# Four loads for six at the end of a row-sum kernel

## The chip, the cores and the metric

The kernel runs on one core of one Trainium2 chip. The metric is the device time of one execution in microseconds (us), taken over several executions.

## The reference

```python
x = randn(32, 512, 1024), float32
out = sum(maximum(x, 0), axis=-1)      # shape (32, 512), float32
```

There are 16,384 rows of 1024 columns, 67.1 MB to read and 0.07 MB to write. Each row is clamped at zero and summed.

## The kernel before

Each of the 128 partitions has 128 rows of its own. Seven loads of 16 rows a partition (8.4 MB each) fill three buffers in turn. The scalar engine (ACT) clamps and the vector engine (DVE) sums. The last 16 rows come in smaller loads, so that little work is left after the last byte. All loads go out on one queue, that of SyncE (SP). Each load has a semaphore, a counter that reaches 16 when all 16 DMA engines have finished their part of the load; an instruction that uses the data waits for 16. That moment is called the landing here.

The parts that the change and the argument touch, with cuts marked:

```python
TAIL = [8, 4, 2, 1]                  # rows of the tail loads, then the last row in pieces:
PIECES = [244, 252, 260, 268]        # columns
# ... cut ...
    extra = len(PIECES) - 1
    parts = [                        # the last piece has room for the sums of the others
        nc.alloc_sbuf_tensor(f"piece{i}", [P, w + extra * (i == extra)], F32)
        for i, w in enumerate(PIECES)
    ]
# ... cut: load() issues on SP and counts up a semaphore of its own by 16; act_row() and
#     dve_row() clamp and sum one row with accum_out, waiting for `loaded` where given ...
    for n in TAIL:
        loaded = load(
            buf[:, c : c + n, :], rows(m, n), None if c else freed[NB - NBUF]
        )
        for i in range(n):           # rows alternate between ACT and DVE
            if i % 2 == 0 or (n == 8 and i == 7):
                act_row(buf[:, c, :], m, loaded if i == 0 else None)
            else:
                dve_row(buf[:, c, :], res[:, m : m + 1], loaded if i == 1 else None)
            c += 1
            m += 1
    col = 0
    arrived = []
    for part, w in zip(parts, PIECES):
        arrived.append(load(part[:, :w], rows(m, 1)[:, 0, col : col + w]))
        col += w

    store(0, ROWS, *freed[0])
    store(ROWS, NT - ROWS - 2, n_act - 1, n_dve)

    last, w = parts[-1], PIECES[-1]
    for i in range(extra):           # the sum of piece i goes into column w + i of the last piece
        dve_row(parts[i][:, :], last[:, w + i : w + i + 1], arrived[i])
    nc.vector.wait_ge(arrived[-1], 16)          # L203: a separate wait instruction
    before_last = n_dve
    nc.vector.tensor_scalar(                    # L205: the last piece and the three sums
        out=last[:, :], in0=last[:, :], scalar1=0.0, scalar2=None,
        op0=MAX, op1=ADD, accum_out=res[:, NT - 1 : NT],
    ).wait_op(sems.dve, before_last, "sem-ge").then_inc(sems.dve, 1)
    n_dve += 1
    store(NT - 2, 2, n_act, n_dve)
```

The last DVE instruction has two things to wait for: the last load and DVE's own earlier sums. The kernel puts the first into an instruction of its own and the second on the instruction itself.

Of the kernel before, what the change touches and what calls it, by code (L numbers as in the profile page):

```python
# [4 lines left out]
F32 = mybir.dt.float32  # L5
RELU = mybir.ActivationFunctionType.Relu
MAX, ADD = mybir.AluOpType.max, mybir.AluOpType.add
P = 128

ROWS = 16  # L10
# [3 lines left out]
TWO = [[16], [16], [16], [8, 8], [8, 8], [7, 7], []]  # L14
ACT = [0, 0, 0, 0, 0, 2, 9]
DVE = [0, 0, 0, 0, 0, 0, 7]

TAIL = [8, 4, 2, 1]
PIECES = [244, 252, 260, 268]

EARLY = 1

# [1 line left out]
def kernel(tc: tile.TileContext, x: bass.AP, out: bass.AP):  # L24
    nc = tc.nc
    sems = Semaphores(tc)

    tc.close()
    tc.compile()
    nc.cur_bb = nc.bb_map[tc.start_bb_name]  # L30
    body = nc.cur_bb.bb.instructions
    ends = list(body)
    body.clear()
    n_stores = relu_sum(nc, sems, x, out)
    body.extend(ends)


    nc.cur_bb = nc.bb_map[tc.start_bb_name + "_end"]
    body = nc.cur_bb.bb.instructions
    clear = semaphore_clear(body)  # L40
    body.clear()
    nc.gpsimd.wait_ge(sems.stored, 16 * n_stores)
    body.extend(clear)
    issue_ahead_of_the_barrier(tc, EARLY)


class Semaphores:
    def __init__(self, tc: tile.TileContext):
        n = len(TWO) + len(TAIL) + len(PIECES)
        self.loads = [tc.alloc_semaphore(f"load{i}") for i in range(n)]  # L50
        self.act = tc.alloc_semaphore("act")
        self.dve = tc.alloc_semaphore("dve")
        self.stored = tc.alloc_semaphore("stored")


def relu_sum(nc, sems: Semaphores, x: bass.AP, out: bass.AP):
    x_flat = x.flatten_outer_dims()
    N, D = x_flat.shape
    NT = N // P
    NB = len(TWO)  # L60
    assert N == P * NT == P * ROWS * (NB + 1)
    assert sum(TAIL) == ROWS - 1 and sum(PIECES) == D

    bufs = [nc.alloc_sbuf_tensor(f"io{i}", [P, ROWS, D], F32) for i in range(NBUF)]
    res = nc.alloc_sbuf_tensor("res", [P, NT], F32)
    extra = len(PIECES) - 1
    parts = [
        nc.alloc_sbuf_tensor(f"piece{i}", [P, w + extra * (i == extra)], F32)
        for i, w in enumerate(PIECES)
    ]  # L70


# [7 lines left out]
    def rows(m, n):  # L80
        if m < ROWS:
            return xf[:, m : m + n, :]
        return xv[:, m - ROWS : m - ROWS + n, :]

    def sums(m, n):
        if m < ROWS:
            return of[:, m : m + n], res[:, m : m + n]
        return ov[:, m - ROWS : m - ROWS + n], res[:, m : m + n]
# [3 lines left out]
    def load(dst, src, after=None):  # L92
        nonlocal n_load
        dma = nc.sync.dma_start(out=dst, in_=src)  # L94
        if after:
            dma.wait_op(sems.dve, after[1], "sem-ge")
        dma.then_inc(sems.loads[n_load], 16)
        n_load += 1
        return sems.loads[n_load - 1]

    def store(m, n, act, dve):
        nonlocal n_store
        dst, src = sums(m, n)
        nc.sync.wait_ge(sems.act, act)
        nc.sync.dma_start(out=dst, in_=src).wait_op(sems.dve, dve, "sem-ge").then_inc(
            sems.stored, 16
        )
        n_store += 1
# [16 lines left out]
    def act_row(ap, m, loaded):  # L125
        nonlocal n_act
        i = nc.scalar.activation(  # L127
            out=ap, in_=ap, func=RELU, accum_out=res[:, m : m + 1]
        )
        if loaded is not None:  # L130
            i.wait_op(loaded, 16, "sem-ge")
        i.then_inc(sems.act, 1)
        n_act += 1

    def dve_row(ap, accum_out, loaded):
        nonlocal n_dve
        i = nc.vector.tensor_scalar(  # L137
            out=ap,
            in0=ap,
            scalar1=0.0,  # L140
            scalar2=None,
            op0=MAX,
            op1=ADD,
            accum_out=accum_out,
        )
        if loaded is not None:
            i.wait_op(loaded, 16, "sem-ge")
        i.then_inc(sems.dve, 1)
        n_dve += 1

    freed = []
    m = 0
    for j in range(NB):
        buf = bufs[j % NBUF]
        loaded = load(buf[:, :, :], rows(m, ROWS), j >= NBUF and freed[j - NBUF])
        c = 0
# [19 lines left out]
    buf = bufs[NB % NBUF]  # L176
    c = 0
# [4 lines that stand above are left out]
        for i in range(n):  # L182
# [3 lines left out]
                dve_row(buf[:, c, :], res[:, m : m + 1], loaded if i == 1 else None)  # L186
            c += 1
            m += 1
    col = 0
    arrived = []  # L190
    for part, w in zip(parts, PIECES):
        arrived.append(load(part[:, :w], rows(m, 1)[:, 0, col : col + w]))
        col += w



    store(0, ROWS, *freed[0])
    store(ROWS, NT - ROWS - 2, n_act - 1, n_dve)

    last, w = parts[-1], PIECES[-1]  # L200
    for i in range(extra):
        dve_row(parts[i][:, :], last[:, w + i : w + i + 1], arrived[i])
    nc.vector.wait_ge(arrived[-1], 16)  # L203
    before_last = n_dve
    nc.vector.tensor_scalar(  # L205
# [3 lines left out]
        scalar2=None,  # L209
        op0=MAX,  # L210
        op1=ADD,
        accum_out=res[:, NT - 1 : NT],
    ).wait_op(sems.dve, before_last, "sem-ge").then_inc(sems.dve, 1)
    n_dve += 1
    store(NT - 2, 2, n_act, n_dve)
# [59 lines left out]
```

## Time and profile before

| | before |
|---|---|
| time, median of 3 runs | 162.18 us (162.17 to 162.97) |
| span in the profile | 160.06 us |
| DVE busy / ACT busy | 74% / 65% |
| DMA packets | 2592, 67.18 MB |

The table of stretches gives, for each stretch, its length, the busy time of DVE, ACT and POOL, then the clock, the busy share of the 16 DMA engines (which can read slightly above 1 in this view) and GB/s. Near the end of before:

```profile
151.00:152.00 1.00, 1.00 (x3) 1.00 (x3) 0.00 (x0) 1.00 0.97 410
153.00:154.00 1.00, 1.00 (x3) 1.00 (x3) 0.00 (x0) 1.00 0.97 410
155.00:156.00 1.00, 0.96 (x1) 0.99 (x2) 0.00 (x0) 1.00 1.02 372
```

In these stretches the DMA engines are busy all the time; DVE and ACT nearly are too, but with work that the loads have just brought.

The timeline of DVE at the end (start, duration, line, instruction, and in brackets idle time before it with what ended it; the long instructions clamp and sum, the short ones that follow read out the sum):

```profile
156.72 0.41 DVE L137 TENSOR_SCALAR_CACHE_REDUCE piece<-piece 128x244 f32<-128x244 f32 x1 [0.44 <-DMA piece<-in_x_dram]
157.05 0.08 DVE L137 DVE_READ_ACCUMULATOR piece<-piece 128x1 f32 x1
157.08 0.42 DVE L137 TENSOR_SCALAR_CACHE_REDUCE piece<-piece 128x252 f32<-128x252 f32 x1
157.42 0.08 DVE L137 DVE_READ_ACCUMULATOR piece<-piece 128x1 f32 x1
157.45 0.43 DVE L137 TENSOR_SCALAR_CACHE_REDUCE piece<-piece 128x260 f32<-128x260 f32 x1
157.80 0.09 DVE L137 DVE_READ_ACCUMULATOR piece<-piece 128x1 f32 x1
157.92 0.43 DVE L205 TENSOR_SCALAR_CACHE_REDUCE piece<-piece 128x271 f32<-128x271 f32 x1
158.28 0.08 DVE L205 DVE_READ_ACCUMULATOR piece<-piece 128x1 f32 x1
```

And the end of the chain of waits (start, duration, what), followed back from the last instruction ("issue" is time in which the engine waited for nothing that the profile shows):

```profile
127.86 28.83 DMA piece<-in_x_dram
156.69 0.02 issue
156.72 1.18 DVE piece L137 x6
157.90 0.03 issue
157.92 0.44 DVE piece L205 x2
```

The chain runs through the first piece's landing and then through DVE alone. The semaphore records of the trace tell when each load has landed on all 16 DMA engines: the four pieces at 156.69, 157.06, 157.43 and 157.80 us.

### The profile page before, as it was taken

What the parts mean: (1) busy time and instruction counts of PE and PEld (TensorE: products, weight loads), DVE (VectorE), ACT (ScalarE), POOL (GpSimd) and SP (SyncE); (2) the same over time, 40 slices, a digit from 0 to 9 for tenths busy, and PEclk for the clock granted to TensorE, in tenths of its full rate; (3) what the DMA queues carried; (4) which work ended last, traced back from release to release, by engine and by line L of the source; (5) the groups of instructions that cost most, each with busy time, mean ns of one, the idle gap of its engine ahead of it and who ended that gap; (6) DMA issues with size and microseconds to landing.
All of it is one profiled execution on the core that took longest, in us unless ns stands there. A gap on an engine that the chain in (4) does not pass through costs nothing.

```text
span 160.1 us, 133 instructions
## 1 busy us (share of the span) xinstructions
DVE 117.7 (74%) x43; ACT 104.2 (65%) x50; POOL 0.2 (0%) x4
## 2 busy tenths in 40 slices
DVE  0000000009999499994999999999999999999994
ACT  3000059990799708995099942999239992599993
POOL 0000000000000000000000000000000000000000
DMA  7996996996996996997998999979969969999993
GB/s 262 524 524 262 524 524 262 524 524 262 524 508 278 524 508 278 524 475 311 524 409 377 524 393 393 524 328 459 524 278 508 524 262 524 393 393 422 409 400 96
DMA packets 2592, 67.18 MB, mean 420 GB/s; under 512 B 672, under 2 KB 1184, under 8 KB 1312
## 3 DMA queue, kind: packets, MB, share of 16 engines
q1 hardware_dynamic: 2592, 67.18, 98.0%
HBM read 67.11 MB, written 0.07 MB: 420 GB/s over the span
## 4 chain that ended last, share of the span: by engine, by line
DMA 43%; DVE 33%; ACT 17%; another core or an unknown queue 3%; SPq 1%; issue 0%
DVE res L120 32%; DMA io<-in_x_dram 25%; DMA piece<-in_x_dram 18%; ACT io L112 17%; SPq L94 1%; DVE piece L137 1%; DVE piece L205 0%
## 5 line engine op out<-in xcount | busy, mean ns | idle before, releaser
L120 DVE TENSOR_REDUCE res<-io 128x8 f32<-128x8192 f32 (+2 forms) x9 | 101.1, 11287 | 40.0 <-ACT io L112 40.0
L112 ACT ACTIVATE io<-io 128x8192 f32<-128x8192 f32 (+2 forms) x9 | 81.7, 9110 | 47.1 <-DMA io<-in_x_dram 47.1
L127 ACT ACTIVATE io<-io 128x1024 f32<-128x1024 f32 x20 | 20.9, 1043 | 5.4 <-DMA io<-in_x_dram 5.3
L137 DVE TENSOR_SCALAR_CACHE_REDUCE io<-io 128x1024 f32<-128x1024 f32 x13 | 15.0, 1214 | 0.2
L127 ACT ACTIVATION_READ_ACCUMULATOR io<-io 128x1 f32 x20 | 3.7, 187 | 0.0
L112 ACT ACT_TABLE_LOAD x1 | 1.3, 1283 | 0.8 <-PEq L259 0.8
L137 DVE TENSOR_SCALAR_CACHE_REDUCE piece<-piece 128x244 f32<-128x244 f32 (+2 forms) x3 | 1.2, 416 | 0.4 <-DMA piece<-in_x_dram 0.4
L137 DVE DVE_READ_ACCUMULATOR io<-io 128x1 f32 x13 | 1.1, 82 | 0.0
L205 DVE TENSOR_SCALAR_CACHE_REDUCE piece<-piece 128x271 f32<-128x271 f32 x1 | 0.4, 435 | 0.0
L137 DVE DVE_READ_ACCUMULATOR piece<-piece 128x1 f32 x3 | 0.3, 84 | 0.0
L259 POOL MEMSET const-bfloat16-1.0<- 128x1 bf16 x1 | 0.1, 101 | 0.0
L259 POOL MEMSET const-uint8-127<- 128x1 uint8 x1 | 0.1, 101 | 0.0
L259 POOL MEMSET const-float32-0.0<- 128x1 f32 x1 | 0.1, 98 | 0.2 <-issue 0.2
L259 POOL MEMSET const-float32-1.0<- 128x1 f32 x1 | 0.1, 98 | 0.0
L205 DVE DVE_READ_ACCUMULATOR piece<-piece 128x1 f32 x1 | 0.1, 82 | 0.0
## 6 DMA issues: line engine op xcount, KB each, us to landing
io<-in_x_dram SPq DMA_DIRECT2D x1, 4096.0 KB, 21.6
io<-in_x_dram SPq DMA_DIRECT2D x1, 2048.0 KB, 26.1
io<-in_x_dram SPq DMA_DIRECT2D x1, 1024.0 KB, 28.1
io<-in_x_dram SPq DMA_DIRECT2D x1, 512.0 KB, 28.9
piece<-in_x_dram SPq DMA_DIRECT2D x1, 134.0 KB, 28.5
piece<-in_x_dram SPq DMA_DIRECT2D x1, 130.0 KB, 28.6
piece<-in_x_dram SPq DMA_DIRECT2D x1, 126.0 KB, 28.7
piece<-in_x_dram SPq DMA_DIRECT2D x1, 122.0 KB, 28.8
```

The lines of the kernel that those rows point to most:

```text
L94: dma = nc.sync.dma_start(out=dst, in_=src)
L112: i = nc.scalar.activation(out=ap, in_=ap, func=RELU)
L120: nc.vector.tensor_reduce(out=res[:, m : m + n], in_=ap, axis=mybir.AxisListType.X, op=ADD).wait_op(sems.act, n_act, "sem-ge").then_inc(se ...
L127: i = nc.scalar.activation(out=ap, in_=ap, func=RELU, accum_out=res[:, m : m + 1])
L137: i = nc.vector.tensor_scalar(out=ap, in0=ap, scalar1=0.0, scalar2=None, op0=MAX, op1=ADD, accum_out=accum_out,)
L205: nc.vector.tensor_scalar(out=last[:, :], in0=last[:, :], scalar1=0.0, scalar2=None, op0=MAX, op1=ADD, accum_out=res[:, NT - 1 : NT],).wai ...
L259: nc = _bacc.Bacc("TRN2", target_bir_lowering=False, num_devices=1)
```

## The change

The intent is to have fewer loads and to let DVE start on the piecewise row earlier. Two rows and the first 360 columns of the third come as one load, then the whole fourth row, which ACT sums meanwhile, then the third row's other 260 and 404 columns. The bytes are the same.

```diff
-TAIL = [8, 4, 2, 1]
-PIECES = [244, 252, 260, 268]
+TAIL = [8, 4]
+PIECES = [360, 260, 404]
 # ... cut: buffers and asserts ...
-    col = 0
+
+    first = PIECES[0]
+    loaded = load(
+        buf[:, :, :].rearrange("p c d -> p (c d)")[:, c * D : (c + 2) * D + first],
+        rows(m, 3).rearrange("p c d -> p (c d)")[:, : 2 * D + first],
+    )
+    act_row(buf[:, c, :], m, loaded)
+    dve_row(buf[:, c + 1, :], res[:, m + 1 : m + 2], loaded)
+    last_loaded = load(buf[:, c + 3, :], rows(m + 3, 1)[:, 0, :])
     arrived = []
-    for part, w in zip(parts, PIECES):
-        arrived.append(load(part[:, :w], rows(m, 1)[:, 0, col : col + w]))
+    col = first
+    for part, w in zip(parts, PIECES[1:]):
+        arrived.append(load(part[:, :w], rows(m + 2, 1)[:, 0, col : col + w]))
         col += w
+    sums_done = n_act, n_dve
+    act_row(buf[:, c + 3, :], m + 3, last_loaded)
 # ... cut ...
-    store(ROWS, NT - ROWS - 2, n_act - 1, n_dve)
+    store(ROWS, NT - ROWS - 2, *sums_done)
 
     last, w = parts[-1], PIECES[-1]
-    for i in range(extra):
-        dve_row(parts[i][:, :], last[:, w + i : w + i + 1], arrived[i])
+    dve_row(buf[:, c + 2, :first], last[:, w : w + 1], None)
+    for i in range(1, extra):
+        dve_row(parts[i - 1][:, :], last[:, w + i : w + i + 1], arrived[i - 1])
     nc.vector.wait_ge(arrived[-1], 16)
 # ... cut: the last instruction is as before, its sum goes to NT - 2 for NT - 1
```

More of the change, by code (lines that the diff above doesn't have):

```diff
@@ L48, in __init__ @@
     def __init__(self, tc: tile.TileContext):
-        n = len(TWO) + len(TAIL) + len(PIECES)
+        n = len(TWO) + len(TAIL) + 1 + len(PIECES)
         self.loads = [tc.alloc_semaphore(f"load{i}") for i in range(n)]
@@ L61, in relu_sum @@
     assert N == P * NT == P * ROWS * (NB + 1)
-    assert sum(TAIL) == ROWS - 1 and sum(PIECES) == D
+    assert sum(TAIL) == ROWS - 4 and sum(PIECES) == D
     bufs = [nc.alloc_sbuf_tensor(f"io{i}", [P, ROWS, D], F32) for i in range(NBUF)]
@@ L67, in relu_sum @@
     parts = [
-        nc.alloc_sbuf_tensor(f"piece{i}", [P, w + extra * (i == extra)], F32)
-        for i, w in enumerate(PIECES)
+        nc.alloc_sbuf_tensor(f"piece{i + 1}", [P, w + extra * (i + 1 == extra)], F32)
+        for i, w in enumerate(PIECES[1:])
     ]
@@ L211, in relu_sum @@
         op1=ADD,
-        accum_out=res[:, NT - 1 : NT],
+        accum_out=res[:, NT - 2 : NT - 1],
     ).wait_op(sems.dve, before_last, "sem-ge").then_inc(sems.dve, 1)
```

## The prediction

> **What bounds it now.** Loading. In the table of stretches the DMA engines are busy for 0.92 to 1.08 of every microsecond from 147 to 157 us; the vector engine (DVE, 74% of the span) and the scalar engine (ACT, 65%) follow the landings at the end. The eight-row and four-row tail loads stay, so everything up to 152.5 us should stay.
>
> **The end, before** (timeline, and semaphore landings in the trace):
> - Landings: four rows 152.53, two rows 155.02, one row 156.31, pieces 156.69, 157.06, 157.43, 157.80 us.
> - Queued tail loads fit a fixed cost plus 1.20 us a row: 9.71 us for 8 rows, 4.90 for 4, 2.49 for 2, 1.29 for 1. So about 0.09 us per load; 0.07 by the last pieces.
> - DVE takes piece 1 on landing (156.72) and is paced by landings until 157.45. The third piece (0.43 us) ends at 157.88, later than the last landing; the last instruction (128x271, 0.435 us) runs from 157.92 to 158.36. The last store goes out at 158.42 and lands 1.4 us later.
>
> This fits the Trainium skill, "DMA: Bandwidth & Descriptors", Queues, rings and completion order: an engine consumes descriptors in ring order[...].
>
> **What the change does.** The bytes are the same; two loads fewer save 0.14 to 0.18 us of load time. DVE has three accumulating instructions at the end for four, and 360 columns of them come early, with the second row. The last DVE instruction grows from 271 to 406 columns.
>
> **Estimate of the new end** (from those numbers, after 152.53):
> - 2408 columns: 2.83 + 0.09, landing 155.45. ACT takes the first row until about 156.65; DVE takes the second from 155.47 in steps of 1.14 us a row, starts the 360 columns at 156.61 and is free at about 157.06.
> - Fourth row: +1.29, 156.74. ACT has it done at about 157.93; not critical.
> - 260 columns: +0.38, 157.12. DVE 157.14 to 157.56, no longer late.
> - 404 columns: +0.55, 157.67. The last DVE instruction starts on landing, 157.69, and takes 0.435 us plus 135 columns at 1.03 ns (slope between 426 ns for 260 columns and 1214 ns for 1024), 0.575 us: end 158.27.
>
> The sum: the last start moves from 157.92 to 157.69 (0.13 us from earlier landing, 0.1 us from DVE no longer being late); 0.14 us goes back to the longer last instruction. Net gain 0.09 us, all on the critical path. The middle store goes out about 0.4 us later, still 1.5 us ahead of the last store, so it should cost nothing.
>
> **Prediction: 162.08 us, range 161.75 to 162.45.** Chances: faster by over 2% 0.01, within 2% 0.98, slower 0.01. The range comes from the spread of runs (162.17 to 162.97) more than from the change.
>
> **What would show it.** Right: the span is about 160.0 us; the last load lands at 157.6 to 157.7; the chain of waits ends with a piece's load, then one DVE instruction of about 0.575 us, without the three earlier pieces; DVE idles some 0.1 us before it; the last store still lands after 1.4 us. Wrong: the four-row load lands at another time; the last load still lands at 157.8 (no fixed cost saved); or the 260 columns start late because the 360 held DVE.
>
> **What would make it wrong.** Loads that start off row boundaries run slower; the later middle store delays the last one; ACT's last row ends after DVE because its load lands over 0.3 us later than estimated; the chip's state moves time by more than 0.1 us.

## More of the kernel before

The page's line on packets, and the timeline of SP (start, duration, what):

```profile
DMA packets 2592, 67.18 MB, mean 420 GB/s; under 512 B 672, under 2 KB 1184, under 8 KB 1312
```

```profile
126.05 1.77 SPq L94 DMA_DIRECT2D io<-in_x_dram  x4
127.86 1.92 SPq L94 DMA_DIRECT2D piece<-in_x_dram  x4
```

The eight tail loads are issued one after another, far ahead, and queue up. The first of them goes out at 126.05 us, and I count the tail from there.

## The result

| | before | after |
|---|---|---|
| time, median of 6 runs | 162.13 us (161.98 to 162.97) | 162.00 us (161.85 to 162.25) |
| ratio after/before | | 0.9986, 95% interval 0.9966 to 1.0006 |
| span in the profile | 160.06 us | 160.06 us |
| DMA packets | 2592 | 2304 |
| first tail load issued | 126.05 us | 126.09 us |
| last landing, after that issue | 31.75 us | 31.58 us |
| last DVE instruction, start after the last landing | 0.12 us | 0.12 us |
| its duration | 0.435 us | 0.577 us |
| end of DVE's work, after that issue | 32.32 us | 32.29 us |

A ratio is the mean time of one kernel's runs over that of the other's runs of the same rounds, so it is not quite the ratio of the medians quoted. The interval contains 1: the times say "the same within 0.35%" and no more. In the traces, the last landings of the four runs with exactly these loads (after, after_again, after_swap, one_wait) lie between 31.55 and 31.59 us, so I take 0.03 us as what the landings resolve. The gain of 0.03 us in the last line is no larger than that, though the second pair of profiles shows it again.

After, the lines that answer to those shown of before. The page's line on packets and SP's timeline:

```profile
DMA packets 2304, 67.18 MB, mean 420 GB/s; under 512 B 640, under 2 KB 896, under 8 KB 1024
```

```profile
126.09 1.77 SPq L96 DMA_DIRECT2D io<-in_x_dram  x4
127.90 1.01 SPq L96 DMA_DIRECT2D piece<-in_x_dram  x2
```

The timeline of DVE at the end:

```profile
155.52 1.22 DVE L139 TENSOR_SCALAR_CACHE_REDUCE io<-io 128x1024 f32<-128x1024 f32 x1 [0.57 <-DMA io<-in_x_dram]
156.67 0.08 DVE L139 DVE_READ_ACCUMULATOR io<-io 128x1 f32 x1
156.67 0.52 DVE L139 TENSOR_SCALAR_CACHE_REDUCE io<-io 128x360 f32<-128x360 f32 x1
157.12 0.08 DVE L139 DVE_READ_ACCUMULATOR io<-io 128x1 f32 x1
157.18 0.42 DVE L139 TENSOR_SCALAR_CACHE_REDUCE piece<-piece 128x260 f32<-128x260 f32 x1
157.53 0.08 DVE L139 DVE_READ_ACCUMULATOR piece<-piece 128x1 f32 x1
157.79 0.58 DVE L219 TENSOR_SCALAR_CACHE_REDUCE piece<-piece 128x406 f32<-128x406 f32 x1 [0.17 <-DMA piece<-in_x_dram]
158.29 0.09 DVE L219 DVE_READ_ACCUMULATOR piece<-piece 128x1 f32 x1
```

And the end of its chain of waits (DVEq is DVE's sequencer):

```profile
128.42 29.25 DMA piece<-in_x_dram
157.67 0.03 issue
157.70 0.02 DVEq L217
157.72 0.07 issue
157.79 0.58 DVE piece L219 x2
```

The chain now runs through the last load. Between its landing at 157.67 and the last DVE instruction at 157.79 lies the separate wait instruction (L217), which ends at 157.72, and then 0.07 us in which the trace shows nothing. DVE had been done since 157.62, so its own earlier sums did not hold it.

Two theories of why the tail gained only 0.03 us:

- **Mine, of the prediction.** In before, DVE was late by 0.1 us, and the last instruction would otherwise have started on landing. The change removed that.
- **The rival.** A separate wait costs about 0.1 us after the landing in both kernels. DVE was not what held before; its late end only happened to coincide with the end of that wait. Then the earlier landing is all that is gained, and the longer last instruction takes it back.

### The profile page after: what moved, and what is told of

Same layout as the page of the kernel before. It is cut to its first block, busy times and chain, and to the rows that moved or that the text cites. A ratio compares the mean times of both kernels' runs of the same rounds, so it can differ in the third digit from the quotient of the medians.

```text
span 160.1 us, 129 instructions
## 1 busy us (share of the span) xinstructions
DVE 117.5 (73%) x41; ACT 104.2 (65%) x50; POOL 0.2 (0%) x4
## 2 busy tenths in 40 slices
DMA packets 2304, 67.18 MB, mean 420 GB/s; under 512 B 640, under 2 KB 896, under 8 KB 1024
## 3 DMA queue, kind: packets, MB, share of 16 engines
q1 hardware_dynamic: 2304, 67.18, 97.8%
## 4 chain that ended last, share of the span: by engine, by line
DMA 44%; DVE 33%; ACT 17%; another core or an unknown queue 3%; SPq 1%; issue 0%; DVEq 0%
DVE res L122 32%; DMA io<-in_x_dram 25%; DMA piece<-in_x_dram 18%; ACT io L114 17%; SPq L96 1%; DVE piece L219 0%; DVEq L217 0%
## 5 line engine op out<-in xcount | busy, mean ns | idle before, releaser
L139 DVE TENSOR_SCALAR_CACHE_REDUCE io<-io 128x1024 f32<-128x1024 f32 (+1 forms) x14 | 15.5, 1173 | 0.6 <-DMA io<-in_x_dram 0.6
L219 DVE TENSOR_SCALAR_CACHE_REDUCE piece<-piece 128x406 f32<-128x406 f32 x1 | 0.6, 577 | 0.2 <-DMA piece<-in_x_dram 0.2
```

Of the source, the lines that this page charges most:

```text
L139: i = nc.vector.tensor_scalar(out=ap, in0=ap, scalar1=0.0, scalar2=None, op0=MAX, op1=ADD, accum_out=accum_out,)
L219: nc.vector.tensor_scalar(out=last[:, :], in0=last[:, :], scalar1=0.0, scalar2=None, op0=MAX, op1=ADD, accum_out=res[:, NT - 2 : NT - 1],) ...
```

## The experiments

Twelve kernels ran. The ten that compute the reference's result were correct and all their timed runs were in the fast state; the two that leave out a piece are wrong on purpose and were run once each, so their state is unknown and only intervals inside their traces are used. In the measured lines, "landing" and "end" are those of the last load and of DVE's last instruction, counted from the issue of the first tail load, as in the table above. "Gap" is from the last landing to the start of the last DVE instruction.

| kernel | landing | gap | end | time, median | ratio to before (95%) |
|---|---|---|---|---|---|
| before, first profile | 31.75 | 0.12 | 32.32 | | |
| before_again | 31.75 | 0.12 | 32.31 | 162.02 | 0.9997 (0.9985 to 1.0010) |
| after, first profile | 31.58 | 0.12 | 32.29 | 162.00 | 0.9986 (0.9966 to 1.0006) |
| after_again | 31.59 | 0.12 | 32.29 | 162.01 | 0.9992 (0.9980 to 1.0005) |
| three_pieces | 31.68 | 0.12 | 32.38 | 162.22 | 1.0011 (0.9998 to 1.0025) |
| unmerged | 31.73 | 0.12 | 32.43 | 162.12 | 0.9998 (0.9985 to 1.0010) |
| after_swap | 31.55 | 0.12 | 32.25 | 161.93 | 0.9991 (0.9978 to 1.0003) |
| skip_third (wrong result) | 31.76 | 0.12 | 32.32 | | |
| skip_swap (wrong result) | 31.75 | 0.02 | 32.22 | | |
| single_rows | 32.44 | 0.12 | 33.14 | 162.86 | 1.0050 (1.0037 to 1.0064) |
| row_packets | 32.33 | 0.12 | 33.03 | 162.75 | 1.0039 (1.0024 to 1.0055) |
| one_wait | 31.58 | 0.02 | 32.19 | 161.91 | 0.9993 (0.9980 to 1.0007) |
| one_wait_sized | 31.54 | 0.05 | 32.15 | 161.75 | 0.9985 (0.9973 to 0.9998) |
| resized | 31.56 | 0.15 | 32.23 | 161.99 | 0.9996 (0.9984 to 1.0009) |

### before_again: the control

The kernel before, unchanged.

> Control: the kernel before, run against itself, to size the noise. Any honest ratio here is 1.000; its scatter says what a difference of 0.1 us (0.06%) is worth. In the profile: last load 5.27 us after the four-row load lands, last DVE instruction 0.12 us after that, 0.435 us long.

The same code, in the same job, had medians of 162.02 and 162.14 us: 0.12 us apart with no difference at all. So no difference of 0.1 us between two medians here is evidence. The intervals in the trace repeated to 0.01 us. What varies is the start: the first tail load was issued between 125.96 and 126.28 us over all the runs' profiles, and the end moves with it. That is why the two spans, both 160.06 us, hide the 0.03 us.

### after_again

The changed kernel, unchanged.

> The changed kernel again, for a tighter interval. Theory of the prediction (DVE no longer late, 0.09 us gained): ratio 0.9994, and from the landing of the four-row load to the end of the last DVE instruction 5.74 us, against 5.83 before. Rival (the last DVE instruction starts about 0.12 us after the last landing in both kernels, so the earlier landing is all that is gained and the longer instruction takes it back): ratio 0.9998 to 1.0000, and 5.80 us as in the first profile.

The end came 32.29 us after the issue as in the first profile, 0.02 to 0.03 us earlier than before. From the landing of the four-row load it came after 5.80 us (152.75 to 158.55), which is the rival's figure and not mine of 5.74. The time's ratio, 0.9992, cannot tell the two apart.

### three_pieces: part of the change alone

```diff
-PIECES = [244, 252, 260, 268]
+PIECES = [360, 260, 404]          # the kernel before, TAIL as it was
```

> One part of the change alone: the kernel before with its last row in three pieces of 360, 260 and 404 columns for four. Both theories: one load fewer, last landing 0.08 us earlier (5.20 us after the four-row landing for 5.27), last DVE instruction 0.577 us for 0.435, so 0.06 to 0.08 us slower in all: ratio 1.0004 to 1.0005. If pieces alone are what gained, it would be faster instead.

The landing came 0.07 us earlier and the end 0.06 us later than before, as expected. Fewer and larger pieces alone lose, because the last instruction is longer. The time (1.0011) leans the same way but its interval contains 1.

### unmerged: the change without its merged load

```diff
-        buf[:, :, :].rearrange("p c d -> p (c d)")[:, c * D : (c + 2) * D + first],
-        rows(m, 3).rearrange("p c d -> p (c d)")[:, : 2 * D + first],
+        buf[:, c : c + 2, :],
+        rows(m, 2),
     )
+    first_loaded = load(buf[:, c + 2, :first], rows(m + 2, 1)[:, 0, :first])
 # ... cut: DVE's 360 columns wait for first_loaded
```

> The change without its merged load: two rows and the 360 columns come as two loads (five for four), in the same order. If each load has a fixed cost of 0.08 us, the last landing comes 5.18 us after the four-row landing (after: 5.10) and the time is 0.08 us more than the changed kernel's, about equal to before: ratio 1.0000 to 1.0004. If loads have no fixed cost, it is as the changed kernel.

One load more made the landing 0.15 us later than in the changed kernel, in the expected direction but nearly twice the expected 0.08 us. Part of that was there before the changed loads: counted from the landing of the four-row load, which the two kernels share, the last landing came after 5.21 us for 5.10, so 0.11 us later. Three_pieces has just as many loads and packets, and by that count it landed after 5.20 us, the same as unmerged. The time did not show the difference.

### single_rows and row_packets: what a load costs

Both change only how the 8-row and 4-row loads come. In single_rows they are twelve loads of one row. In row_packets each is two loads of every second row, so that a partition's rows are not contiguous and each row is a packet of its own.

```diff
-TAIL = [8, 4]
+TAIL = [1] * 12                   # single_rows
 # ... cut: rows stay with the engine they had, each waits for its own load
```

```diff
-        loaded = load(
-            buf[:, c : c + n, :], rows(m, n), None if c else freed[NB - NBUF]
-        )
+        half = [                    # row_packets
+            load(
+                buf[:, c + k : c + n : 2, :],
+                rows(m, n)[:, k::2, :],
+                None if c or k else freed[NB - NBUF],
+            )
+            for k in range(2)
+        ]
 # ... cut: each row waits for its half
```

> The changed kernel with its 8-row and 4-row tail loads as twelve loads of one row: ten loads more and 80 packets more per DMA engine. With a fixed cost of 0.08 to 0.09 us a load, by load or by packet, the last landing moves 0.8 to 0.9 us later and the time with it: ratio about 1.005. If queued loads overlap and have no fixed cost, nothing moves.

> The changed kernel with its 8-row and 4-row tail loads each as two loads of every second row, so that rows are not contiguous: two loads more, and as many packets of 4096 bytes as in single_rows (80 more per DMA engine). If the fixed cost lies in packets (about 9 ns each), the last landing moves 0.7 to 0.8 us later, nearly as in single_rows; if it lies in loads, only 0.17 us later.

The lines on packets, first of single_rows, then of row_packets:

```profile
DMA packets 3744, 67.18 MB, mean 417 GB/s; under 512 B 800, under 2 KB 1056, under 8 KB 2720
```

```profile
DMA packets 3616, 67.18 MB, mean 418 GB/s; under 512 B 672, under 2 KB 928, under 8 KB 2592
```

Single_rows has 1440 packets more than the changed kernel, 90 on each of the 16 engines, and landed 0.86 us later (32.44 for 31.58): 9.5 ns a packet. Row_packets has 1312 more, 82 an engine, with only two loads more, and landed 0.75 us later: 9.1 ns a packet. Ten loads or two loads make little difference; the packets count. Every load of before and after has one packet for each of the 128 partitions and one 4-byte packet on each engine for the semaphore, 144 in all: 2592 less 2304 is twice that. So the "fixed cost of a load" of the prediction is 9 packets an engine at 9.1 to 9.5 ns, or 0.08 to 0.09 us, and the change's two loads come to 0.16 to 0.17 us, as much as its landing came earlier. The times agree: here even the intervals against before (1.0037 to 1.0064, 1.0024 to 1.0055) lie clear of 1.

The packets' own durations show it too: in before, a 4096-byte packet took 159 ns and an 8192-byte one 309 ns (medians), so twice the first is 9 ns more than the second. The Trainium skill, "DMA: Bandwidth & Descriptors", Measured, gives about 10.5 ns a packet for the smallest transfers issued from GpSimd. The 9.1 and 9.5 ns of these loads, queued from SP, are near it, but they are the extra time of one more packet for the same bytes, not the whole time of a small packet.

### skip_third: was DVE late in before?

The kernel before, without DVE's sum of its third piece. The load stays, so the landings stay.

```diff
-    for i in range(extra):
+    for i in range(extra - 1):
 # ... cut: the last instruction covers 270 columns for 271
```

> Wrong result on purpose: the kernel before without the DVE instruction for its third piece; the load stays. DVE is then free about 0.4 us before the last landing. Prediction's theory (DVE late by 0.1 us in the kernel before): the last DVE instruction starts 0.02 us after the last landing (157.80 to 157.82), 0.1 us earlier than before. Rival (the landing and the separate wait hold it): it starts 0.12 us after the last landing as before, and the end does not move.

The timeline of DVE and the chain of waits of skip_third:

```profile
157.22 0.42 DVE L137 TENSOR_SCALAR_CACHE_REDUCE piece<-piece 128x252 f32<-128x252 f32 x1
157.56 0.08 DVE L137 DVE_READ_ACCUMULATOR piece<-piece 128x1 f32 x1
158.06 0.43 DVE L205 TENSOR_SCALAR_CACHE_REDUCE piece<-piece 128x270 f32<-128x270 f32 x1 [0.42 <-DMA piece<-in_x_dram]
```

```profile
157.94 0.03 issue
157.97 0.02 DVEq L203
157.99 0.07 issue
158.06 0.44 DVE piece L205 x2
```

DVE is free from 157.64 us, 0.30 us ahead of the last landing at 157.94. Even so its last instruction starts 0.12 us after the landing, and its end is 32.32 us after the issue, as before. So taking DVE's third sum away gains nothing: in before it was not the only thing that held the last instruction. My theory, by which this was worth 0.1 us, falls here.

### after_swap and skip_swap: the separate wait

Both exchange the two waits: DVE's own sums are waited for in the separate instruction, and the last instruction itself waits for the last load. After_swap is the changed kernel; skip_swap is skip_third.

```diff
-    nc.vector.wait_ge(arrived[-1], 16)
     before_last = n_dve
+    nc.vector.wait_ge(sems.dve, before_last)
 # ... cut ...
-    ).wait_op(sems.dve, before_last, "sem-ge").then_inc(sems.dve, 1)
+    ).wait_op(arrived[-1], 16, "sem-ge").then_inc(sems.dve, 1)
```

> The changed kernel with the two waits ahead of the last DVE instruction exchanged: the wait on DVE's own earlier sums becomes the separate instruction, and the last instruction itself waits for the last load. Rival (a separate wait instruction costs about 0.1 us after the landing): the last DVE instruction starts 0.02 to 0.04 us after the last landing for 0.12, and all ends 0.08 to 0.10 us earlier: ratio about 0.9993. Prediction's theory (start on landing; the 0.1 us seen is something else, such as the landing being seen late): start stays 0.12 us after the landing and nothing changes.

After_swap's gap stayed at 0.12 us, which on the face of it speaks against the rival. But the test was badly built: DVE's sum of 260 columns ended at 157.67 us, the landing was at 157.68, so the separate wait, now for DVE, was released at the same moment as before, and the last instruction came at 157.80. The exchange had only moved the cost to the other of two paths of equal length. That called for a case in which one of them is early:

> Wrong result on purpose, as skip_third, with the two waits ahead of the last DVE instruction exchanged. DVE is free 0.3 us before the last landing here, so the separate wait is over long before. If a separate wait instruction costs 0.1 us after what it waits for, the last DVE instruction now starts 0.02 to 0.04 us after the last landing (0.12 in skip_third). If the 0.12 us lies in the landing itself, it stays at 0.12.

```profile
157.87 0.02 issue
157.89 0.44 DVE piece L205 x2
```

In skip_swap the separate wait was over at 157.63 (by the trace's record of that instruction), and the last instruction started at 157.89, 0.02 us after the landing at 157.87. The same work, the same landing, two waits exchanged: 0.12 became 0.02 us. This shows the rival's cost; one_wait, below, shows it again in a kernel that computes the right result.

The Trainium skill, "Perfetto Trace Analysis", Per-engine timelines, fits it: an instruction that only waits holds the sequencer, and the next is fetched and decoded only after it, while a DVE instruction that waits for itself has been decoded before and stands in a wait queue. The page gives no duration. Here the difference was 0.10 us.

### one_wait, one_wait_sized and resized: using it

In one_wait, DVE's two earlier sums count up the last load's own semaphore, so that a single wait for 16 + 2 on the last instruction covers both:

```diff
-        i.then_inc(sems.dve, 1)
-        n_dve += 1
+        i.then_inc(done or sems.dve, 1)         # done: the last load's semaphore for the two sums
+        n_dve += done is None
 # ... cut ...
-    nc.vector.wait_ge(arrived[-1], 16)
-    before_last = n_dve
 # ... cut ...
-    ).wait_op(sems.dve, before_last, "sem-ge").then_inc(sems.dve, 1)
+    ).wait_op(arrived[-1], 16 + extra, "sem-ge").then_inc(sems.dve, 1)
```

One_wait_sized has in addition `PIECES = [360, 284, 380]`. Resized is the changed kernel with its two waits as they were and `PIECES = [360, 328, 336]`.

> The changed kernel with one wait ahead of its last DVE instruction: the two earlier sums of DVE count up the last load's semaphore, and the last instruction waits for 16 + 2. If the separate wait was the cost: it starts 0.02 to 0.04 us after the last landing for 0.12, and ends 0.08 to 0.09 us earlier: 5.71 us after the four-row landing for 5.80, ratio about 0.9989 where the changed kernel has 0.9992 to 0.9996. If the landing itself holds it: no change.

> As one_wait, with the third row in 360, 284 and 380 columns: the last instruction is 24 columns shorter (0.552 us), the piece before it ends just as the last load lands. Ends about 0.02 us ahead of one_wait, 5.69 us after the four-row landing, too little for the times to show. If the piece before it ends later than the landing, the gain is lost.

> The changed kernel with both its waits as they were, and the third row in 360, 328 and 336 columns. The last landing stays, the piece before the last ends about when the separate wait does, and the last instruction takes 0.51 us for 0.577: ends 5.73 us after the four-row landing for 5.80, ratio 0.0004 below the changed kernel's. If DVE is then late instead, up to 0.05 us less.

One_wait's gap was 0.02 us and its end 0.10 us earlier than the changed kernel's, counted from the issue. The end of its chain of waits, which has no DVEq line any more:

```profile
157.73 0.02 issue
157.75 0.58 DVE piece L217 x2
```

One_wait_sized ended 0.04 us ahead of that, where 0.02 us was expected; its last landing came 0.04 us earlier, about what such landings scatter. Its DVE timeline:

```profile
157.08 0.45 DVE L139 TENSOR_SCALAR_CACHE_REDUCE piece<-piece 128x284 f32<-128x284 f32 x1
157.46 0.08 DVE L139 DVE_READ_ACCUMULATOR piece<-piece 128x1 f32 x1
157.57 0.55 DVE L217 TENSOR_SCALAR_CACHE_REDUCE piece<-piece 128x382 f32<-128x382 f32 x1
```

The sum of 284 columns ended at 157.54, the last load landed at 157.53: both paths arrive together. It is the fastest kernel, 161.75 us against 162.00 us for before in the same job, and the only one faster than before by an interval that excludes 1, by 0.15%. With nine such intervals near 1 in the table, one that just misses 1 is weak evidence by itself. Of its 0.25 us, the tail explains 0.17 us (32.15 for 32.32); its profile also started the tail early (125.99), which is scatter. Resized ended 0.06 us ahead of the changed kernel, as expected (0.07), although its 328-column sum was now just late: it ended at 157.96 and the last instruction began at 158.00.

## Why the prediction was right or wrong

The time was right: 162.08 us was predicted, with a range of 161.75 to 162.45, and 162.00 us was measured. That says little: the range also holds the 162.13 us of before, so a change that did nothing would have fallen in it as well. Nor did the signs listed in the prediction test its weakest step. The last load landed at 157.67, the chain ended as foretold, DVE idled for 0.17 us before its last instruction, and all of this came out right beside a step that failed. The mechanism was right in two of three terms, and the sum was too high by a factor of about three.

- **Everything up to the four-row load stays.** Right: that load landed at 152.53 and 152.57 us, and the issue of the first tail load had moved by the same 0.04 us, which is scatter.
- **Two loads fewer save 0.14 to 0.18 us of load time, so the last landing moves 0.13 us earlier.** Right in kind: it came 0.17 us earlier counted from the issue (31.75 to 31.58), 0.04 us more than estimated and at the upper end of the load time. By the two packet tests it consists of 18 packets an engine, at 9.1 to 9.5 ns each.
- **The last DVE instruction grows by 0.14 us.** Right: 0.435 to 0.577 us.
- **"0.1 us from DVE no longer being late".** This is the step that failed. It was worth nothing: the gap from landing to start was 0.12 us in before and 0.12 us in after, and skip_third shows that it stays so when DVE is free 0.3 us early. What held the last instruction in after was the separate wait instruction, which my estimate of the new kernel left out ("starts on landing, 157.69"; it was 157.79): with it gone, in one_wait, the gap is 0.02 us. In before, DVE's third sum was indeed late (157.88), but the end of the delay behind the separate wait fell within a few hundredths of a microsecond of it, and the chain of waits showed only the sum. Removing the sum left the other; no run removed the wait from before with all its sums in place.
- **Net gain.** Predicted 0.09 us. Measured from the issue: 0.17 earlier landing, less 0.14 longer instruction, 0.03 us (32.32 to 32.29). The missing 0.1 us was in part made up, by luck, by the 0.04 us more in the landing. The gain is too small for the times, where the control differed from itself by 0.12 us.
- **The later middle store and ACT's last row cost nothing.** Right: the last store landed 1.40 us after its issue in both (158.39 to 159.79, 158.40 to 159.80), and ACT was done at 157.97, ahead of DVE's 158.37.

## What to carry to other kernels

When two paths end within a few hundredths of a microsecond, the chain of waits names one of them; before calling it the limit, take it away (even at the cost of a wrong result) and see whether the end moves. Where an instruction must wait for two things, let the one that comes last be the wait on the instruction itself, or count both on one semaphore (0.02 us for 0.12 us here). For queued loads count packets (partitions times contiguous runs, and the semaphore's) and not loads, and for effects under 0.1% compare intervals inside traces, with a control of the same kernel beside itself.

## What the Trainium skill lacked or had wrong

- "Perfetto Trace Analysis", Per-engine timelines, describes the wait queue and a sequencer-only instruction but gives no cost. Here a DVE instruction started 0.02 us after the load that it waited for itself, and 0.12 us after it behind a separate wait instruction (skip_swap and skip_third).
- "DMA: Bandwidth & Descriptors", Measured, has about 10.5 ns a packet for the smallest transfers issued from GpSimd; it has no measured time a packet for loads queued from SP. Here 82 and 90 packets more on an engine cost 9.1 and 9.5 ns each, with 4096-byte packets.
- The same section's table gives 341 GB/s for a 1 MB transfer issued from GpSimd, though by my arithmetic the 6.15 us in the same row would make about 170 GB/s, half of that. Here a 0.5 MB load (one row of each partition), queued from SP behind others, landed 1.29 us after the one ahead of it, which is about 405 GB/s. No run here times a load by itself.
